# Merged plan of a two-layer diffusion block: the scheduler prices DVE beside GpSimd, and its priorities change

## The chip, the cores and the metric

The kernel runs on one core of a Trainium2 chip. The metric is the device time of one execution in microseconds (us). Engines are named as in the profile: PE is TensorE's matmul, PEld its weight load, DVE is VectorE, ACT is ScalarE, POOL is GpSimd, and SP issues most transfers.

## The reference, cut to what matters

Layer 0 is windowed attention and an MLP, layer 1 a Griffin recurrence and an MLP, over 1024 latent tokens and 256 context tokens of width 1024. The change lies in layer 0's MLP and, above all, in layer 1's recurrent mixer:

```python
def rglru_coeffs(u, w_a, b_a, w_i, b_i, lam):          # five blocks of 256 channels
    r = sigmoid(einsum('btnk,nkj->btnj', ub, w_a) + b_a)
    i = sigmoid(einsum('btnk,nkj->btnj', ub, w_i) + b_i)
    log_a = -LRU_C * softplus(-lam) * r
    return exp(log_a), sqrt(-expm1(2 * log_a)) * (i * u)

def rglru_mixer(h_x, h_c, w_in, conv_w, conv_b, w_a, ..., w_out):
    w_gate, w_rec = w_in[:, :D_RNN], w_in[:, D_RNN:]      # D_RNN = 1280
    u_x = centred_dwconv(h_x @ w_rec, conv_w, conv_b)     # four taps
    u_c = centred_dwconv(h_c @ w_rec, conv_w, conv_b)
    for d in range(2):                                    # two directions
        a_c, bx_c = rglru_coeffs(u_c, ...)
        _, hc_last = linear_scan(a_c, bx_c, 0, rev)       # h = a * h + bx
        a_x, bx_x = rglru_coeffs(u_x, ...)
        ys_x, _ = linear_scan(a_x, bx_x, hc_last, rev)
    return (gelu(h_x @ w_gate) * (ys_x[0] + ys_x[1])) @ w_out
```

Around each mixer and MLP stand RMS norms and adaLN shift, scale and gate.

## The kernel before

Each float32 product is made of three matmuls (lines 249 to 251) of operands split into a high part, which is a rounding copy, and a low part, which is a subtraction. So PE reads nothing that ACT, DVE or POOL has not split first.

No order is written by hand. A `Plan` collects operations with `add`: the engines that may run one, its cost on each, a priority key (lower goes first), what it depends on, and the buffer slots that it takes and frees. `any` adds one that two or three engines may run. `order` walks the list with a clock for each engine: of the operations that can start, it takes the one that starts first, keys deciding among those that start within `eps` of it; a second choice of engine must not end more than `alt` later than the first would; a change of ACT's function table adds `tab` to the key. `cal` scales the costs, and `bus` spaces transfers. `emit` then writes the instructions out in that order, and each engine's instructions run on the chip in the order written, held only by semaphores. An operation of `when` is a pseudo transfer: it moves nothing, and frees slots or delays what depends on it.

There are four plans. The third, merged one holds layer 0's MLP (`layer0_mlp`), layer 1's mixer and the start of layer 1's MLP (`middle`). Its keys are `KEYS2`. In this text:

- u step m (0 to 9), `plan_in`: one 128-channel column of `h @ w_rec`. Three products of PE (tile `pf`, reading `h` and `w`), one for the 256 context tokens (group 2) and one for each latent half (groups 0 and 1); a copy to `prec` and `pre`; the convolution on DVE (lines 1883 and 1887), 12 instructions for a step.
- gate step, `plan_in` too: the same with `w_gate`, gelu on ACT (tile `gp`, line 1921), ten for each latent half.
- block n.d (n 0 to 4, direction d 0 or 1), `plan_rec`: 12 products (tile `pg`, 72 matmuls), 12 sigmoids, exponential, tanh and square root on ACT, the splits of `u` (lines 1958 to 1967), squares, products (lines 2047 to 2079) and scans (line 2087) on DVE, some on POOL.
- output, `plan_proj`: ten groups of eight products with `w_out` (tile `py`), each added into `y` by DVE (line 1681). `plan_residual` and `plan_hgen` then make the next MLP's input (lines 1625 to 1655, and 1579 to 1593), whose first products are `plan_cols` of `middle` and `plan_seven`.

Keys of `KEYS2` used below: u step m has `a0 + ap*m`, its second latent half `al` more; gate steps `g0` or `g1` plus `gp*m`; block n.d `c0 + (2n+d)*cp`; the output `w0`; the next MLP `r0`.

Of the kernel before, what the change touches and what calls it, by code (L numbers as in the profile page):

```python
# [12 lines left out]
ALU = mybir.AluOpType  # L13
# [5 lines left out]
D = 1024  # L19
# [23 lines left out]
class Plan:  # L43
# [4 lines left out]
    def __init__(self, slots, keys, start={}):  # L48
        self.keys = keys
        self.start = start  # L50
        self.free = {s: [(0.0, "DMA", q) for q, m in (n if isinstance(n, list) else [(None, n)]) for _ in range(m)]
                     for s, n in slots.items()}
        self.ops = []
        self.got = {}
        self.cal, self.base = keys.get("cal"), 0.0


    def add(self, eng, ns, key, fn, deps=(), take=(), free=(), tab=None):
        many = not isinstance(eng, str)
# [22 lines left out]
    def order(self):  # L82
# [8 lines left out]
        open_ = {e: [] for e in self.LAT}  # L91
        free = self.free
        tab = None
        bus = 0.0
        for i, o in enumerate(ops):
            if not wait[i]:
                for e, ns in o[0]:
# [2 lines left out]
        eps = self.keys["eps"]  # L100
# [13 lines left out]
        while len(at) < len(ops):  # L114
            best = None
            for e, c in open_.items():
                ts = []
                for i in c:
                    t = first(i, e)
                    if t is None:  # L120
                        continue
                    o = ops[i][0]
                    if len(o) > 1 and o[0][0] != e:
                        if t + dict(o)[e] > first(i, o[0][0]) + o[0][1] + slack:
                            continue
                    ts.append((t, i))
                if not ts:
                    continue
                lim = min(ts)[0] + eps.get(e, 0)
                k, t, i = min((ops[i][1] + (pen if ops[i][6] not in (None, tab) else 0), t, i) for t, i in ts if t <= lim)  # L130
                if best is None or t < best[0]:
                    best = t, i, e
            if best is None:
                raise RuntimeError("plan is stuck: " + str([(ops[i][0], ops[i][1], ops[i][4]) for c in open_.values() for i in c]))
            t, i, eng = best
            opts, key, fn, deps, take, fr, tb, _ = ops[i]
            for e, ns in opts:
                open_[e].remove(i)
            self.got[i] = [(s, free[s].pop(0)[2]) for s in take]
            f = t + dict(opts)[eng]  # L140
            if eng == "DMA" and dict(opts)[eng] >= 2000 and self.keys.get("bus"):
                bus = max(t, bus) + self.keys["bus"] * (1 if dict(opts)[eng] > 2300 else 0.5)
                f = max(f, bus + 1500)
            if tb is not None and tb != tab and eng == "ACT":
                tab = tb
                f += 1283
            if eng != "DMA":
                end[eng] = f
            for x in fr:
# [49 lines left out]
class Body:  # L199
    KEYS = {'ctx': 0.706, 'kv': 0.956, 'q': -1.4, 'S': -0.826, 'dS': 0.182, 'v': 0.068, 'e': 0.292, 'n': -0.211, 'tp': 0.197, 'dt': 0.205, 'a': 0.087, 'pv': 0.593, 'o': 0.343, 'w': 0.695, 'dw': 0.162, 'r': 0.664, 'eps': {'ACT': 143.51971938059006, 'Pool': 265}}  # L200
    KEYS0 = {'cr': 32.6, 'x': [2.69, 4.49, -4.04, -3.82, 11.07, 11.46, 13.54, 8.52, 59.28, 46.73], 'a0': 6.01, 'ad': 4.7, 'ac': 7.11, 'cp': [1, 0, 0, 0, 1, 1, 0, 1, 1, 1, 1, 1, 0, 1, 0, 0], 'w': [2.18, 62.63, 75.38], 'wd': [13.74, 0.3, 15.36], 'h': [-24.73, 13.55, 40.24], 'hd': [3.18, 5.2, 4.18], 'tl': 19.32, 'blocks': [[[0, 1, 2, 3, 4, 5], [6, 7], [8, 9]], [[0, 1, 2], [3, 4], [5, 6], [7, 8, 9]], [[8, 9, 0], [1], [2], [3]]], 'cq': [1, 0, 0, 1, 0, 1, 0, 1, 1, 1, 1, 0, 0, 0, 0, 1, 1, 0, 1, 1, 0, 1, 1, 1], 'p': [32.68, -6.89, 47.14, 3.71, 20.15, -8.8, 64.94], 'pd': 7.27, 'p1': 82.17, 'qk': -8.12, 'k': 144.05, 'g': [45.38, 61.79, 109.14], 'gd': [5.61, 8.84, 15.66], 'alt': 1800, 'eps': {'Q': 0, 'PE': 0, 'Pool': 44, 'DVE': 27, 'ACT': 0}}
    KEYS3 = dict(r=3, alt=200, bus=2300, eps=dict(DVE=100))
    KEYS2 = dict(m=(2.3, 0.68, 10.54), p=(7.5, 1.52, 9.72), h=(10.4, 11.24, 37.3), pi=0.66, a0=28.64, ap=9.33, al=-5.36, g0=155.5,
                 g1=151.7, gp=4.73, c0=98.5, cp=2.33, w0=312.9, wp=16.6, r0=389.52, spill=5, tab=122.87, alt=72.5, ba=8, bb=6, bw=9, bg=7,
                 bo=0, hm=1, cal=1, bus=2300, eps=dict(DVE=20, ACT=0, Pool=48))
# [1406 lines left out]
    def plan_residual(self, p, key, t, ys, yop, xs, xop, G, put, norm):  # L1612
# [25 lines left out]
        for n in range(2):  # L1638
            g.append(p.any(PAIR(512), "DVE Pool", key, lambda e, n=n: e.tensor_tensor(
                out=y(n), in0=y(n), in1=G["G"][:, n * 512:(n + 1) * 512], op=ALU.mult), [sq[n], G["op"]]))  # L1640
            o.append(p.add("DVE", 665, key, lambda n=n: nc.vector.scalar_tensor_tensor(  # L1641
                out=x(n), in0=y(n), scalar=z["a"][:, 2:3], in1=x(n), op0=ALU.mult, op1=ALU.add), [r, g[n], xop]))
        z["g"] = g
        if not norm:
            for n in range(2):
# [207 lines left out]
    def plan_in(self, p, E, h, hop, hold):  # L1853
# [5 lines left out]
        for m in range(NR):  # L1859
# [36 lines left out]
                    tap(i, z["c"][:, 0], z["c"][:, 1])  # L1896
            o = u0 = p.add("DVE", 750, key, c0, [es[1]], take=["t"])
            for i in (0, 1, 3):
                o = p.add("DVE", 1200, key, lambda i=i, z=z, tap=tap: tap(i, z["x"], z["u"]), [o], free=[(es[0], 0)] if i == 3 else [])
            c = p.add("DVE", 1950, key, cc, [es[2]])  # L1900

            def store(m=m, z=z):
# [30 lines left out]
    def plan_rec(self, p, E):  # L1933
# [4 lines left out]
        for n in range(NB):  # L1938
# [32 lines left out]
            for kt in range(2):  # L1971
                lu.append(p.add("DMA", 2500, K - 4, load(kt), deps, take=["t"]))
                c = p.add("DVE", 800, K - 4, split_c(kt), [luc], take=["s"])
                a = p.add("DVE", 605, K - 4, split(kt, 0), [lu[kt]], take=["t"])
                b = p.add("DVE", 1140, K - 4, split(kt, 1), [a], take=["t"])
                uop += [c, a, b]
                uhold += [(c, 0), (a, 0), (b, 0)]
            yt, yhold = {}, {}
            for d in range(2):
# [51 lines left out]
                for jt in range(2):  # L2031
                    for c in (1, 0):
# [28 lines left out]
                        st[jt, c] = p.add("DVE", sz * 1.04 + 70, q, f_st, [b, w_], free=[(w_, 0)])  # L2061
# [7 lines left out]
                for jt in range(2):  # L2069
                    for c in (1, 0):  # L2070
# [143 lines left out]
```

## Time and profile before

| | |
|---|---|
| median of three runs | 2858.9 us (2858.09 to 2860.35) |
| profiled execution: own time, span of its instructions | 2859.99 us, 2858.2 us |
| PE busy | 2673.9 us, 94% of the span |
| DVE busy | 2127.6 us, 74% |
| ACT, POOL busy | 1107.5 us (39%), 851.0 us (30%) |
| mean granted PE clock | 0.972 of full speed |

Shares are means over stages of very different kinds; the merged plan's PE work lies from about 670 to 2243 us. 1.8 us of the execution lie outside the span.

### The profile page before, as it was taken

The numbers are of one execution on the slowest core, as the hardware profiler recorded it, in microseconds if no ns is written. First come the engines' busy times: TensorE is split into PE (matmuls) and PEld (weight loads), VectorE is DVE, ScalarE is ACT, GpSimd is POOL, SyncE is SP. The second block draws the span as 40 slices with busy tenths as digits, with TensorE's granted clock in tenths as the row PEclk, the third lists the DMA queues.
The fourth block names the chain that finished last, engine by engine and source line by source line (L and its number), as shares of the span: only waits on it lengthen the run. The fifth ranks groups of instructions, "written<-read, shape, count | busy, mean of one in ns | idle before, by whom it ended". The sixth has DMA issues, their size and how long they took to land. (4 is left out here: it accounts for less than half of the span.)

```text
span 2858.2 us, 35048 instructions
## 1 busy us (share of the span) xinstructions
PE 2673.9 (94%) x12886; PEld 2205.4 (77%) x12886; DVE 2127.6 (74%) x3178; ACT 1107.5 (39%) x2040; POOL 851.0 (30%) x720
## 2 busy tenths in 40 slices
PE   6798999998999999999998999978896999999997
PEld 4677788877788888888887887756675888888886
DVE  8988999996876666765668677799988666655546
ACT  5326777775322223111115245776525212221111
POOL 7643444443311110100116022355435111101113
PEclk9899999999999999999999999988998999999999
DMA  6462321224233334454552223334331323333323
GB/s 233 157 218 83 110 78 45 68 65 163 74 121 105 129 129 159 155 169 140 168 177 81 92 78 98 136 125 155 139 112 63 110 100 111 133 126 110 102 83 125
DMA packets 115332, 345.03 MB, mean 121 GB/s; under 512 B 12836, under 2 KB 15828, under 8 KB 115160
## 3 DMA queue, kind: packets, MB, share of 16 engines
q1 hardware_dynamic: 111704, 330.21, 34.2%
q10 hardware_dynamic: 3456, 12.58, 1.1%
q8 instruction: 101, 1.65, 0.2%
q14 instruction: 71, 0.58, 0.1%
HBM read 254.37 MB, written 88.38 MB: 120 GB/s over the span
## 5 line engine op out<-in xcount | busy, mean ns | idle before, releaser
L251 PE MATMUL pf<-h,w 128*128 128x512 f32 (+1 forms) x1400 | 517.5, 370 | 23.7 <-POOL w L1525 17.4
L250 PE MATMUL pf<-h,w 128*128 128x512 f32 (+1 forms) x1400 | 516.2, 369 | 9.8 <-DVE h L1593 9.5
L249 PE MATMUL pf<-h,w 128*128 128x512 f32 (+1 forms) x1400 | 516.6, 369 | 5.5 <-ACT h L1583 2.8
L1500 DVE TENSOR_TENSOR y<-y,py 128x512 f32<-128x512 f32 x268 | 183.0, 685 | 274.4 <-PE py L251 273.8
L251 PEld LDWEIGHTS pf<-h,w 128*128 128x128 f32 x1400 | 267.8, 191 | 70.5 <-POOL w L1525 20.0
L250 PEld LDWEIGHTS pf<-h,w 128*128 128x128 f32 x1400 | 267.8, 191 | 56.2 <-DVE h L1593 13.0
L249 PEld LDWEIGHTS pf<-h,w 128*128 128x128 f32 x1400 | 268.0, 191 | 50.7 <-ACT w L244 3.3
L244 ACT CAST w<-raw 128x1024 fp32r<-128x1024 f32 x142 | 148.4, 1049 | 325.2 <-PE pf L251 107.5
L249 PE MATMUL py<-hw,hw 128*128 128x512 f32 x592 | 230.4, 389 | 0.0
L251 PE MATMUL py<-hw,hw 128*128 128x512 f32 x592 | 230.3, 389 | 0.0
L250 PE MATMUL py<-hw,hw 128*128 128x512 f32 x592 | 230.3, 389 | 0.0
L244 ACT CAST hw<-raw 128x512 fp32r<-128x512 f32 x113 | 69.2, 621 | 391.3 <-DMA raw<-in_w 154.3
L1473 POOL TENSOR_TENSOR hw<-raw,hw 128x512 fp32r<-128x512 f32 x46 | 65.3, 1422 | 489.3 <-DVE hw L244 337.9
L1003 POOL TENSOR_SCALAR P<-P,sc 128x640 f32<-128x640 f32 (+2 forms) x160 | 118.5, 753 | 179.7 <-DVE sc L1000 92.2
L249 PE MATMUL py<-w,hw 128*128 128x512 f32 x432 | 169.0, 391 | 0.0
L250 PE MATMUL py<-w,hw 128*128 128x512 f32 x432 | 168.6, 390 | 0.0
L251 PE MATMUL py<-w,hw 128*128 128x512 f32 x432 | 168.4, 390 | 0.0
L1092 PE MATMUL py<-w,oT 128*128 128x512 f32 x480 | 147.5, 412 | 2.5 <-DVE w L927 1.8
L986 ACT ACTIVATE P<-S,sc 128x640 f32<-128x640 f32 (+2 forms) x160 | 113.9, 712 | 52.8 <-DVE sc L980 35.5
L1473 DVE TENSOR_TENSOR hw<-raw,hw 128x512 fp32r<-128x512 f32 x156 | 116.5, 769 | 20.1 <-ACT hw L244 18.4
L249 PEld LDWEIGHTS py<-hw,hw 128*128 128x128 f32 x592 | 111.1, 188 | 23.2
L251 PEld LDWEIGHTS py<-hw,hw 128*128 128x128 f32 x592 | 111.1, 188 | 23.1
(297 smaller groups left out, 6412.7 us busy)
## 6 DMA issues: line engine op xcount, KB each, us to landing
raw<-in_w SPq DMA_DIRECT2D x128, 512.0 KB, 3.5
raw<-in_ada_t SPq DMA_DIRECT2D x96, 512.0 KB, 3.8
raw<-hid_d SPq DMA_DIRECT2D x64, 512.0 KB, 4.0
hid_d<-c SPq DMA_DIRECT2D x112, 256.0 KB, 2.3
raw<-in_w_in SPq DMA_DIRECT2D x30, 512.0 KB
x<-x_d SPq DMA_DIRECT2D x26, 512.0 KB, 5.6
x_d<-x SPq DMA_DIRECT2D x24, 512.0 KB, 2.8
q_d<-qd ACTq DMA_DIRECT2D x20, 512.0 KB, 4.3
```

The source lines that it names most:

```text
L244: (e.copy if e is self.nc.scalar else e.tensor_copy)(out=out, in_=x)
L249: mm(o, lhsT=lh, rhs=rh, start=start, stop=False, skip_group_check=on)
L250: mm(o, lhsT=lh, rhs=rl, start=False, stop=False, skip_group_check=on)
L251: mm(o, lhsT=ll, rhs=rh, start=False, stop=stop, skip_group_check=on)
L986: nc.scalar.activation(out=z["P"][j][:, :n], in_=z["S", j][:, 256:256 + n], func=AF.Exp, scale=0.125, bias=negm[:, j:j + 1], accum_out=l[: ...
L1003: nc.gpsimd.tensor_scalar(out=z["P"][j][:, :n], in0=z["P"][j][:, :n], scalar1=z["sc"][3][:, j:j + 1], scalar2=1.0, op0=ALU.mult, op1=ALU.mult)
L1092: nc.tensor.matmul(z["ps", n], lhsT=oT[k // 2][2]["oT"][:, x, k % 2], rhs=Wo[k][:, w, n * 512:(n + 1) * 512], start=m == 0, stop=m == 3 * ...
L1473: e.tensor_tensor(out=z[n][:, 1], in0=z["raw"][:, s], in1=z[n][:, 0].bitcast(F32), op=ALU.subtract)
L1500: nc.vector.tensor_tensor(out=y, in0=y, in1=z["ps"], op=ALU.add)
```

## The change

`order` learns that a DVE operation with two operands in SBUF takes longer while POOL has an operation of that kind: by up to 0.43 of its cost, and 0.3 of the time that POOL still needs. Operations that DVE or POOL may run are marked by themselves, and some DVE ones by `two=True`. Pseudo transfers no longer count on the bus. The price is in force only in the merged plan, where `cal` is set. `KEYS2` gets other numbers.

```diff
-    def add(self, eng, ns, key, fn, deps=(), take=(), free=(), tab=None):
+    def add(self, eng, ns, key, fn, deps=(), take=(), free=(), tab=None, two=False):
...
+        if two or many and "Pool" in eng and "DVE" in eng:
+            self.two.add(len(self.ops))
...
-            f = t + dict(opts)[eng]
-            if eng == "DMA" and dict(opts)[eng] >= 2000 and self.keys.get("bus"):
+            d = dict(opts)[eng]
+            if i in self.two and self.cal:
+                if eng == "Pool":
+                    pool = t + d
+                elif eng == "DVE" and pool > t:
+                    d += min(0.43 * d, 0.3 * (pool - t))
+            f = t + d
+            if eng == "DMA" and key > -1e8 and d >= 2000 and self.keys.get("bus"):
...
-    KEYS2 = dict(m=(2.3, 0.68, 10.54), p=(7.5, 1.52, 9.72), h=(10.4, 11.24, 37.3), pi=0.66, a0=28.64, ap=9.33, al=-5.36, g0=155.5,
-                 g1=151.7, gp=4.73, c0=98.5, cp=2.33, w0=312.9, wp=16.6, r0=389.52, spill=5, tab=122.87, alt=72.5, ba=8, bb=6, bw=9, bg=7,
+    KEYS2 = dict(m=(1.7, 5.11, -1.71), p=(-1.36, -6.72, 11.35), h=(15.55, 3.89, 35.01), pi=0.41, a0=28.64, ap=3.48, al=16.78, g0=158.15, g1=151.09,
+                 gp=1.49, c0=134.15, cp=4.74, w0=285.16, wp=16.6, r0=353.51, spill=5, tab=541.22, alt=150, ba=7, bb=7, bw=8, bg=9, bo=0, hm=1, cal=1,
...
-                o = p.add("DVE", 1200, key, lambda i=i, z=z, tap=tap: tap(i, z["x"], z["u"]), [o], free=[(es[0], 0)] if i == 3 else [])
+                o = p.add("DVE", 1200, key, lambda i=i, z=z, tap=tap: tap(i, z["x"], z["u"]), [o], free=[(es[0], 0)] if i == 3 else [], two=True)
```

`two=True` also stands at the residual's last addition, at the splits of `u`, and at the recurrence's products and scans. No operation is added or removed. The instructions of the merged plan change their order, and 266 of its operations change their engine. The changed file is ten lines longer where the mixer stands, so a line L2005 of before is L2015 now.

What the scheduler made of it shows at three places. First PE, where block 0.0 begins, before: three rows of a context product of u step 3, then the block's first product, and u step 4 behind a third of the block.

```order
L249 MATMUL pf_14415<-h_13813,w_14306 128x256
L250 MATMUL pf_14415<-h_13813,w_14306 128x256
L251 MATMUL pf_14415<-h_13813,w_14306 128x256
L249 MATMUL pg_14458<-uhc_14381,w_13979 128x256
L250 MATMUL pg_14458<-uhc_14381,w_13979 128x256
L251 MATMUL pg_14458<-uhc_14381,w_13979 128x256
```

The same place of PE's order now: the rows ahead are the last product of u step 9 (a latent half, 512 columns).

```order
L259 MATMUL pf_14996<-h_14115,w_14874 128x512
L260 MATMUL pf_14996<-h_14115,w_14874 128x512
L261 MATMUL pf_14996<-h_14115,w_14874 128x512
L259 MATMUL pg_15039<-uhc_14502,w_13975 128x256
L260 MATMUL pg_15039<-uhc_14502,w_13975 128x256
L261 MATMUL pg_15039<-uhc_14502,w_13975 128x256
```

The recurrence's first product moved behind all ten u steps; gate steps, two to three beside each block, stand between the blocks now, and behind block 3.1 groups of output products.

Second DVE, at the scans of block 0.0 (order prints a scan as a SCALAR_TENSOR_TENSOR of line 2087), before: the convolution of u step 8 still follows them.

```order
L2087 SCALAR_TENSOR_TENSOR gi_2312_14450<-ga_2313_14451,grc_2317_14455,gi_2312_14450 128x1024
L2087 SCALAR_TENSOR_TENSOR gi_2315_14453<-ga_2316_14454,grc_2318_14456,gi_2315_14453 128x1024
L1883 TENSOR_SCALAR prec_15069<-prec_15069,small 128x256
L1887 SCALAR_TENSOR_TENSOR prec_15069<-prec_15069,small 128x254
L1887 SCALAR_TENSOR_TENSOR prec_15069<-prec_15069,small 128x255 x2
L1883 TENSOR_SCALAR u_15150<-pre_15066,small 128x1024
```

DVE at the end of the u steps now: the last convolution of all, two low parts of weights, and then the first products of block 0.0.

```order
L1893 TENSOR_SCALAR u_15067<-pre_14930,small 128x1024
L1535 TENSOR_TENSOR w_15117<-raw_15086,w_15117 128x1024
L2065 TENSOR_TENSOR grc_2367_15037<-grc_2367_15037,uc_14461 128x256
L2065 TENSOR_TENSOR gi_2364_15034<-gi_2364_15034,u_14466 128x1024
L2057 TENSOR_TENSOR gw_15179<-gac_15038 128x256
```

All convolutions stand ahead of the recurrence's products and scans on DVE now; of its work only the splits of the first `u` are earlier.

Third PE again, where block 4.0 begins. Before, a gate step's last product of the second latent half precedes it.

```order
L249 MATMUL pf_16981<-h_14149,w_16945 128x512
L250 MATMUL pf_16981<-h_14149,w_16945 128x512
L251 MATMUL pf_16981<-h_14149,w_16945 128x512
L249 MATMUL pg_17036<-uhc_16851,w_16788 128x256
L250 MATMUL pg_17036<-uhc_16851,w_16788 128x256
```

Now output products (`py`, reading `z`) precede it, the first twenty of them.

```order
L259 MATMUL py_17242<-w_17200,z_16897 128x512
L260 MATMUL py_17242<-w_17200,z_16897 128x512
L261 MATMUL py_17242<-w_17200,z_16897 128x512
L259 MATMUL pg_17261<-uhc_17044,w_16978 128x256
L260 MATMUL pg_17261<-uhc_17044,w_16978 128x256
```

Block 4.0 moved behind two and a half of the ten output groups; before, it stood ahead of all.

## Rows read from the trace of the kernel before

**Rows 1.** The page: granted PE clock in 40 slices of 71.5 us, in tenths.
```profile
PEclk9899999999999999999999999988998999999999
```

**Rows 2.** Windows: length; busy us of PE, PEld, DVE, ACT, POOL; clock; DMA share, GB/s.
```profile
660.00:760.00 100.00, 88.13 (x451) 72.97 (x449) 73.11 (x87) 47.95 (x83) 41.91 (x31) 0.97 0.36 134
760.00:1482.00 722.00, 720.21 (x3494) 609.25 (x3493) 485.01 (x699) 142.07 (x223) 82.36 (x67) 1.00 0.42 139
1482.00:1548.00 66.00, 62.02 (x292) 51.59 (x291) 57.63 (x93) 35.09 (x77) 39.36 (x46) 0.97 0.41 158
1548.00:1615.00 67.00, 62.36 (x321) 52.66 (x320) 50.38 (x66) 23.58 (x39) 14.91 (x13) 0.95 0.28 97
1615.00:1764.00 149.00, 138.91 (x681) 117.08 (x680) 116.18 (x113) 60.83 (x85) 42.73 (x17) 0.97 0.25 86
1764.00:1834.00 70.00, 70.00 (x332) 58.80 (x331) 39.68 (x37) 48.78 (x65) 13.29 (x7) 1.00 0.38 125
1834.00:1898.00 64.00, 53.79 (x226) 42.96 (x225) 60.39 (x55) 47.75 (x63) 26.59 (x15) 0.88 0.34 120
1898.00:1983.00 85.00, 66.07 (x257) 52.19 (x257) 81.03 (x69) 58.15 (x77) 47.26 (x21) 0.83 0.45 154
1983.00:2167.00 184.00, 151.85 (x669) 123.73 (x668) 156.72 (x187) 86.78 (x150) 82.90 (x68) 0.92 0.36 127
2167.00:2243.00 76.00, 67.39 (x290) 54.03 (x288) 56.51 (x63) 30.49 (x49) 29.53 (x18) 0.96 0.13 48
```

**Rows 3.** The waits of PE, 1482 to 2243 us: total, times, longest.
```profile
PE pf L251 <- POOL w L1525: 17.4, 6, 4.7
```

**Rows 4.** PE in order of time: start, length (pipelined: read the starts), operation.
```profile
1482.16 0.39 PE L250 MATMUL py<-hw,hw 128*128 128x512 f32 x1
1482.39 0.39 PE L251 MATMUL py<-hw,hw 128*128 128x512 f32 x1
...
1547.32 0.60 PE L1579 MATMUL ph<-ident,y 128*128 128x128 f32 x4
...
1615.26 0.28 PE L249 MATMUL pg<-uhc,w 128*128 128x256 f32 x1
1615.38 0.28 PE L250 MATMUL pg<-uhc,w 128*128 128x256 f32 x1
```

**Rows 5.** DVE's groups, 1482 to 2243 us: count, busy us, mean ns, idle before.
```profile
L1681 DVE TENSOR_TENSOR y<-y,py 128x512 f32<-128x512 f32 x84 | 56.0, 680 | 15.2 <-PE py L251 14.9
L1525 DVE TENSOR_TENSOR w<-raw,w 128x1024 fp32r<-128x1024 f32 x39 | 52.1, 1339 | 14.0 <-ACT w L244 13.8
L2087 DVE TENSOR_TENSOR_SCAN gi<-ga,grc,gi 128x1024 f32<-128x1024 f32 x10 | 30.0, 3020 | 0.0
L1887 DVE SCALAR_TENSOR_TENSOR u<-pre,small,u 128x1023 f32<-128x1023 f32 x20 | 28.0, 1406 | 0.4
L2079 DVE TENSOR_TENSOR gi<-gi,gr 128x1024 f32<-128x1024 f32 x20 | 27.4, 1375 | 2.4 <-ACT gr L2075 2.4
L1887 DVE SCALAR_TENSOR_TENSOR prec<-prec,small 128x255 f32<-128x255 f32 x20 | 11.9, 595 | 0.7
L1883 DVE TENSOR_SCALAR u<-pre,small 128x1024 f32<-128x1024 f32 x10 | 10.1, 1012 | 16.4 <-ACT pre L244 16.4
L1883 DVE TENSOR_SCALAR prec<-prec,small 128x256 f32<-128x256 f32 x10 | 10.0, 999 | 1.6 <-ACT prec L244 1.1
L1887 DVE SCALAR_TENSOR_TENSOR prec<-prec,small 128x254 f32<-128x254 f32 x10 | 7.2, 723 | 0.4
```

**Rows 6.** One meeting of DVE and POOL, in order of time.
```profile
1737.40 2.60 POOL L1525 TENSOR_TENSOR w<-raw,w 128x1024 fp32r<-128x1024 f32 x1 [5.38 <-ACT w L244]
...
1737.70 3.38 DVE L2079 TENSOR_TENSOR gi<-gi,gr 128x1024 f32<-128x1024 f32 x1
...
1741.94 1.19 DVE L2079 TENSOR_TENSOR gi<-gi,gr 128x1024 f32<-128x1024 f32 x1
```

**Rows 7.** POOL's group of low weight parts, 1482 to 2243 us.
```profile
L1525 POOL TENSOR_TENSOR w<-raw,w 128x1024 fp32r<-128x1024 f32 x15 | 53.9, 3596 | 140.0 <-ACT w L244 118.5 <-DVE w L244 11.6 <-issue 9.0
```

More of the change, by code (lines that the diff above doesn't have):

```diff
@@ L55, in __init__ @@
         self.cal, self.base = keys.get("cal"), 0.0
-    def add(self, eng, ns, key, fn, deps=(), take=(), free=(), tab=None):
+        self.two = set()
+    def add(self, eng, ns, key, fn, deps=(), take=(), free=(), tab=None, two=False):
         many = not isinstance(eng, str)
@@ L93, in order @@
         tab = None
-        bus = 0.0
+        bus = pool = 0.0
         for i, o in enumerate(ops):
@@ L202 @@
     KEYS3 = dict(r=3, alt=200, bus=2300, eps=dict(DVE=100))
-    KEYS2 = dict(m=(2.3, 0.68, 10.54), p=(7.5, 1.52, 9.72), h=(10.4, 11.24, 37.3), pi=0.66, a0=28.64, ap=9.33, al=-5.36, g0=155.5,
-                 g1=151.7, gp=4.73, c0=98.5, cp=2.33, w0=312.9, wp=16.6, r0=389.52, spill=5, tab=122.87, alt=72.5, ba=8, bb=6, bw=9, bg=7,
-                 bo=0, hm=1, cal=1, bus=2300, eps=dict(DVE=20, ACT=0, Pool=48))
+    KEYS2 = dict(m=(1.7, 5.11, -1.71), p=(-1.36, -6.72, 11.35), h=(15.55, 3.89, 35.01), pi=0.41, a0=28.64, ap=3.48, al=16.78, g0=158.15, g1=151.09,
+                 gp=1.49, c0=134.15, cp=4.74, w0=285.16, wp=16.6, r0=353.51, spill=5, tab=541.22, alt=150, ba=7, bb=7, bw=8, bg=9, bo=0, hm=1, cal=1,
+                 bus=2300, eps={'DVE': 20, 'ACT': 50, 'Pool': 50})
     def __init__(self, tc, A, out, dbg=None, stop=None):
@@ L1641, in plan_residual @@
             o.append(p.add("DVE", 665, key, lambda n=n: nc.vector.scalar_tensor_tensor(
-                out=x(n), in0=y(n), scalar=z["a"][:, 2:3], in1=x(n), op0=ALU.mult, op1=ALU.add), [r, g[n], xop]))
+                out=x(n), in0=y(n), scalar=z["a"][:, 2:3], in1=x(n), op0=ALU.mult, op1=ALU.add), [r, g[n], xop], two=True))
         z["g"] = g
@@ L1973, in plan_rec @@
                 c = p.add("DVE", 800, K - 4, split_c(kt), [luc], take=["s"])
-                a = p.add("DVE", 605, K - 4, split(kt, 0), [lu[kt]], take=["t"])
-                b = p.add("DVE", 1140, K - 4, split(kt, 1), [a], take=["t"])
+                a = p.add("DVE", 605, K - 4, split(kt, 0), [lu[kt]], take=["t"], two=True)
+                b = p.add("DVE", 1140, K - 4, split(kt, 1), [a], take=["t"], two=True)
                 uop += [c, a, b]
@@ L2060, in plan_rec @@
                         ex[jt, c] = b
-                        st[jt, c] = p.add("DVE", sz * 1.04 + 70, q, f_st, [b, w_], free=[(w_, 0)])
+                        st[jt, c] = p.add("DVE", sz * 1.04 + 70, q, f_st, [b, w_], free=[(w_, 0)], two=True)
                         iu[jt, c] = p.any(PAIR(sz), "Pool DVE", q, f_iu, [sg[jt, 1, D]] if c else [sg[jt, 1, 0], sg[jt, 1, 512]])
@@ L2081, in plan_rec @@
                         x = p.add("ACT", sz * 0.833 + 93, q, f_sqrt, [st[jt, c]] + list(ex.values()), tab="sqrt")
-                        bb[jt, c] = p.add("DVE", sz * 1.04 + 70, q, f_b, [x, iu[jt, c]], free=[] if c else [own["r%d" % jt]])
+                        bb[jt, c] = p.add("DVE", sz * 1.04 + 70, q, f_b, [x, iu[jt, c]], free=[] if c else [own["r%d" % jt]], two=True)
                     def f_scan(lo, hi, c, jt=jt, view=view, sl=sl, d=d, t=t):
@@ L2091, in plan_rec @@
                     q = K + 3.5 + 0.3 * jt
-                    x = p.add("DVE", 600, q, f_scan(0, 256, 1), [bb[jt, 1]])
+                    x = p.add("DVE", 600, q, f_scan(0, 256, 1), [bb[jt, 1]], two=True)
                     if d == 0:
-                        x = p.add("DVE", 2130, q, f_scan(0, D, 0), [x, bb[jt, 0]], free=[own["a%d" % jt]])
+                        x = p.add("DVE", 2130, q, f_scan(0, D, 0), [x, bb[jt, 0]], free=[own["a%d" % jt]], two=True)
                         sc[jt] = [x, x]
                     else:
-                        x = p.add("DVE", 1140, q, f_scan(512, D, 0), [x, bb[jt, 0]])
-                        sc[jt] = [p.add("DVE", 1140, q, f_scan(0, 512, 0), [x], free=[own["a%d" % jt]]), x]
+                        x = p.add("DVE", 1140, q, f_scan(512, D, 0), [x, bb[jt, 0]], two=True)
+                        sc[jt] = [p.add("DVE", 1140, q, f_scan(0, 512, 0), [x], free=[own["a%d" % jt]], two=True), x]
                 p.when([sc[0][0], sc[1][0]], [own["rc0"], own["rc1"], own["ac"]])
```

## The prediction

> **What bounds the kernel now.** I read the granted clock along the span first: it falls below nine tenths near the start, from 1858 to 2001 us and from 2144 to 2215 us [rows 1]. Then the windows, cut where PE begins a stage [rows 2]. The merged plan begins with 12 us of PE idle in 660 to 760 us; from 760 to 1482 us PE idles 1.8 of 722 us. Whatever the change moves there is hidden by full PE, so the stage from 1482 to 2243 us decides: 761 us.
>
> What must PE do in it? A matmul of 512 columns follows the one before after 0.23 us, one of 256 after 0.12 us [rows 4]; over a long run I take 0.2267. Counted in the order of PE: two hundred and forty matmuls end the old MLP (54.4 us); a u step has 48 wide and 24 narrow ones, 13.8 us; so has a block; a gate step has 24 wide, 5.44 us, twenty of them 108.8; eighty output products of six, 108.8. With the transposes (four take between 0.33, their starts' distance, and 0.60 us [rows 4]) and the next MLP's first products it is 623 us. So 138 of 761 us are lost on PE.
>
> DVE is busy for 619 of the 761 us, the sum of its column [rows 2], and unevenly: 40 of 70 us in 1764 to 1834, where PE is full, but 60 of 64, 81 of 85 and 157 of 184 us from 1834 to 2167, where PE loses 10, 19 and 32 us and the clock is 0.83 to 0.92. In these three windows DVE is the bound; ahead of them PE mostly is. In PE's order of before, ten of the twenty gate steps, which load PE and hardly DVE, stand beside blocks 0.1 and 1.0, and ten are left for the seven later ones.
>
> **What the change does to each stretch.** I worked with two sums. PE's is the count of matmuls above. DVE's: I walked its order, before and now, up to the last instruction that the first matmul of the stretch needs, directly or through others, buffers to be freed included, and gave each instruction the mean of its group [rows 5], the smaller groups in the same way. The stretches end where the block named starts; c1 is the first product of the next MLP. In us, PE / DVE:
>
> - to block 0.0: before 118.2 / 126.3, took 133; now 200.8 / 176.4
> - to block 1.0: before 133.2 / 117.1, took 149; now 71.0 / 69.5
> - to block 2.0: before 69.7 / 52.1, took 70; now 54.8 / 47.4
> - to block 3.0: before 45.2 / 65.2, took 64; now 54.7 / 58.2
> - to block 4.0: before 53.4 / 71.5, took 85; now 65.6 / 94.4
> - to c1: before 141.1 / 167.8, took 184; now 112.6 / 128.5
> - to the end of the plan: before 62.0 / 52.5, took 76; now 63.3 / 63.0
>
> What each stretch took is the length of its windows [rows 2]. The first one grows because all u steps stand ahead of block 0.0: six of them, 6 x 13.8 = 82.6 us of PE. On DVE that brings 15 long taps forward (x 1.36 us, the mean of the rows of 128x1023 and its sister of 128x1022), seven context convolutions ((10.0 + 11.9 + 7.2) / 10 = 2.9 us each), six first taps (1.01), nine low parts of weights (1.22), less 7.6 us of small work that moves the other way: 50 us [rows 5].
>
> In all, DVE's sums come to 652.5 us before and 637.4 now (means of single instructions, which overlap a little with the next: 5% above the busy 619, on both sides). The difference is choices of engine: the low parts of 12 u and gate weights go from POOL to DVE, those of ten weights the other way; eight products of `i` with `u` go to POOL, eleven to DVE; all the rest nets to a few us.
>
> **The sum.** First stretch: PE bounds it now, 200.8 us, and I keep the loss of before, 133 - 118.2 = 14.8 us. 215.6. From block 0.0 to c1 the larger of the two sums, stretch by stretch, is 133.2 + 69.7 + 65.2 + 71.5 + 167.8 = 507.4 before, which took 552 us: 1.088 of it. Now it is 71.0 + 54.8 + 58.2 + 94.4 + 128.5 = 406.9, and x 1.088 that is 442.7. End: 63.3 and the loss of before, 76 - 62, makes 77.3. Together 735.6 us against 761: 25.4 us less. The profiled execution took 2859.99 us, so 2834.6; it lies 1.1 us above the median of the three runs, so about 2834 on their scale.
>
> Costed at nothing: the attention stage, which another plan orders; layer 1's MLP behind the plan, with the same order as before; and 660 to 1482 us. There PE's order changes for a few products, one context product now needing 27 us of DVE work where PE has 25; cover gone, it costs 3 us. Pseudo transfers off the bus let four loads of `xn` and the first MLP weights change places on SP; I take 1 us either way for nothing.
>
> **Bounds.** The loss of the first stretch: between nothing and 30 us, what PE had lost by block 1.0 (133 + 149 - 251.4). Six waits of PE for a low part made by POOL cost 17.4 us before [rows 3], because such a part takes POOL 3.6 us [rows 7] against DVE's 1.3; in the u and gate steps 14 were POOL's and seven are now. Half of that wait may go: -9, taken as nothing. The factor 1.088: from 1.04 to 1.15, inside the spread of the single stretches, 0.98 to 1.19 (-20, +25).
>
> DVE against POOL: in the meeting shown, DVE's product of 128x1024 began 0.3 us after POOL's subtraction and ended 1.1 us after it, 3.38 us where a free one takes 1.19 [rows 6]. It did not slow down, it stood still. The new price would give it 0.43 x 1.2 = 0.5 us at most, against 2.2 lost. The Trainium skill ("SBUF — State Buffer", section "SBUF: two separate sides") says the same: the port pair that the two engines share is locked for a whole instruction, and the other one blocks. By that rule the plan is still too hopeful wherever the two meet, and DVE will come later than the plan puts it. My sum doesn't use the planned times: the means of rows 5 hold the meetings of before. POOL's work beside DVE's from block 0.0 to c1, counted alike, is 0.45 of DVE's before and 0.49 now; if the stretching follows, DVE's sum there grows by 2%, +8 us. If the new keys keep half of the meetings apart, the products of 128x1024 show what is to be had: 1.375 us on the mean where the free one takes 1.19 [rows 5, 6], a seventh of their time; I take a tenth of DVE's sum, -40, as the far end.
>
> **The rivals.** (a) *DVE's backlog, slower.* The u steps leave DVE 24 us of idle time ahead of block 0.0 (200.8 - 176.4), where before two blocks filled it; behind it 398 us of DVE work wait (its sums from 0.0 to c1 without the choice of the larger). If DVE can't be kept fed there, because the sigmoids, square roots and table loads of one block hold up the next, the order loses. It decides at 468 us for that stretch (761 - 215.6 - 77.3), so at DVE rows worth 0.85 of the time. Before, this ratio was 473.7 / 552 = 0.858 over the whole stretch, but 356.6 / 403 = 0.885 from block 1.0 on, and 304.5 / 333 = 0.914 from block 2.0 on, where DVE was really the bound. At 0.82 it would be 485 us, 17 more than before: about 2876. Against it: before each block from 0.0 to 3.1 PE has 20 to 50 us more to do than DVE, counted from 1482, where before the lead sank to nothing by block 3.1; it is gone only at 4.0.
>
> (b) *Nothing changes.* DVE's total falls by 15 us only; were DVE as full over the stage as before (652.5 / 761 = 0.857), the stage would take 744, and with the 8 us of more meetings 752: 9 us less; with a bad first stretch none. 2850 to 2858.
>
> (c) *Much faster.* Meetings kept apart and the waits for POOL's low parts gone: 442.7 - 40 - 9 and the rest as above gives 2785.
>
> **How the numbers follow.** Forecast, 60%: 2834, its own range 2815 to 2850. (c) in part or whole, 14%. (a) 17%. (b) 9%. The range for 8 in 10 goes from 2802 to 2864: it cuts the far ends of (a) and (c). A measurement of this kernel tells about 0.2%, 5.7 us, from no change. Faster by more: the forecast, (c) and a little of (b), 75%; within: 9%; slower: 16%.
>
> **What would show it.** Right: PE nearly full from the first `pf` of the u steps to the first `pg`, which starts some 215 us after the old MLP's last chunk begins; then PE and DVE both over 85% busy, with no window like 1898 to 1983; c1 some 658 us after the same point (before 685); fewer waits of PE for low parts of POOL. Wrong: DVE idle over 12% between first `pg` and c1, waiting for ACT; PE waiting at block 4.0, where the lead is gone, for splits or a freed tile; or DVE's means above those of rows 5.

## The result, and the profile after

The changed kernel takes 2838.4 us (median of four runs, 2834.5 to 2842.6), the one before 2859.6 us in the same comparison (2858.1 to 2862.8): ratio 0.9925, 95% interval 0.9907 to 0.9942, 21 us less. The profiled execution took 2837.45 us, its span is 2835.7.

The granted clock along the span, in 40 slices of 70.9 us: among the blocks it falls below nine tenths in two slices (1914 to 2056 us), as before ([rows 1], 1858 to 2001 us); the slice at the end of the plan, 2144 to 2215 us before, no longer does.

```profile
PEclk9899999999999999999999999998899999999999
```

The windows of the changed kernel, cut where the rows of [rows 2] are cut: the old MLP's last chunk, the u steps, then from block 0.0 to 1.0, 2.0, 3.0, 4.0, c1 and the plan's last product.

```profile
1485.40:1546.90 61.50, 60.04 (x285) 49.51 (x283) 55.14 (x79) 33.24 (x76) 36.71 (x43) 1.00 0.40 149
1546.90:1696.00 149.10, 145.02 (x757) 124.67 (x758) 95.36 (x125) 41.16 (x74) 17.90 (x18) 0.98 0.27 96
1696.00:1772.20 76.20, 73.09 (x338) 60.87 (x337) 65.63 (x58) 54.01 (x71) 31.13 (x14) 0.98 0.36 118
1772.20:1827.70 55.50, 55.19 (x265) 46.13 (x263) 41.25 (x36) 46.39 (x62) 22.35 (x10) 1.00 0.40 132
1827.70:1897.00 69.30, 60.61 (x265) 49.07 (x266) 67.49 (x58) 48.66 (x66) 44.60 (x19) 0.93 0.45 149
1897.00:1991.70 94.70, 72.80 (x313) 58.23 (x312) 94.53 (x86) 66.58 (x95) 48.70 (x26) 0.87 0.37 133
1991.70:2138.30 146.60, 120.21 (x538) 98.05 (x536) 118.44 (x142) 70.61 (x120) 65.73 (x48) 0.92 0.34 117
2138.30:2219.00 80.70, 72.09 (x297) 57.29 (x298) 66.39 (x69) 34.97 (x62) 48.28 (x35) 0.91 0.20 71
sum 733.60, PE 659.05 PEld 543.84 DVE 604.23 ACT 395.60 POOL 315.40; mean PE 82.38 PEld 67.98 DVE 75.53 ACT 49.45 POOL 39.42
```

The stage takes 733.6 us, where it took 760 (1482.6 to 2242.8): 26.6 less. Of that 2.8 us are lost ahead of it, where it now begins at 1485.4, and 1.3 in the MLP behind it (2219.0 to the end, 616.7 us, and 615.4 before). From block 0.0 to c1 it is 442.3 us now, 551.9 before; up to block 0.0 210.6 us, 132.7 before. One window is still as full on DVE as 1898 to 1983 us was: from block 3.0 to 4.0 DVE works 94.5 of 94.7 us and PE 72.8.

PE shows the gain in two halves. Counted to the end of PE's work in the plan, the stage takes 736.0 us against 762.7. PE idles 74.5 us of it against 88.6, and the same 3060 matmuls keep it busy for 661.5 us against 674.1, at a mean granted clock of 0.94 against 0.93.

PE's waits from block 0.0 to c1, longest totals (total, times, longest):

```profile
PE py L259 <- DVE y L1691: 11.7, 3, 7.4
PE pg L259 <- DVE y L1691: 10.9, 1, 10.9
PE pg L259 <- ACT grc L2015: 9.8, 2, 7.0
PE py L260 <- DVE w L1535: 6.2, 1, 6.2
PE pg L260 <- DVE uh L1970: 4.3, 2, 3.1
```

The u and gate products (`pf`), which waited 17.4 us for POOL's low parts of weights [rows 3], do so no longer. What PE waits for most now is DVE. The wait of 10.9 us shows how, in order of time, at block 4.1 (the rows between are left out at the dots):

```profile
2021.66 0.39 PE L261 MATMUL py<-w,z 128*128 128x512 f32 x1
2023.18 7.00 POOL L1535 TENSOR_TENSOR w<-raw,w 128x1024 fp32r<-128x1024 f32 x2
2023.69 8.64 DVE L2097 TENSOR_TENSOR_SCAN gi<-ga,grc,gi 128x1024 f32<-128x1024 f32 x2
...
2032.25 1.85 DVE L1691 TENSOR_TENSOR y<-y,py 128x512 f32<-128x512 f32 x3
2032.96 0.58 PE L259 MATMUL pg<-uhc,w 128*128 128x256 f32 x1 [10.91 <-DVE y L1691]
```

PE's last output product is done at 2022; the addition that takes it out of PE's result tile, 0.7 us of work, stands on DVE behind two scans, and these take 4.3 us each beside two low parts of weights on POOL (3.0 us was their mean before [rows 5]). Until the addition is done, block 4.1 cannot begin.

What DVE itself waits for from block 0.0 to c1, before:

```profile
DVE y L1681 <- PE py L251: 14.7, 25, 0.7
DVE u L1883 <- ACT pre L244: 14.3, 2, 7.2
DVE w L1525 <- ACT w L244: 13.8, 4, 4.2
DVE pre L244 <- PE pf L251: 12.3, 2, 8.0
DVE gi L2055 <- ACT gi L2005: 9.9, 5, 2.5
DVE grc L2055 <- ACT grc L2005: 6.7, 3, 4.1
```

The same now:

```profile
DVE gi L2065 <- ACT gi L2015: 16.5, 7, 3.8
DVE grc L2065 <- ACT grc L2015: 14.4, 6, 3.9
DVE y L1691 <- PE py L261: 6.0, 11, 1.0
DVE w L1535 <- ACT w L254: 3.1, 3, 1.6
```

The two kinds of waits of the u steps (`pre`, `u`: 26.6 us) are gone, since no u step stands between the blocks. Those for weights and outputs fall from 28.5 to 9.1 us; those for sigmoids (`gi`, `grc`) rise from 16.6 to 30.9. DVE idles 551.9 - 453.8 = 98.1 us there before and 442.3 - 387.3 = 55.0 now. In the stretch ahead, where PE is full, DVE now idles 60 us instead of 25; most of that are ten waits for ACT's copy of a u step's context part:

```profile
DVE prec L1893 <- ACT prec L254: 42.9, 10, 7.7
```

So over the whole stage DVE idles 129.5 us now and 142.5 before.

Three of DVE's groups over the stage, and POOL's low parts, which answer to [rows 5] and [rows 7]:

```profile
L1535 DVE TENSOR_TENSOR w<-raw,w 128x1024 fp32r<-128x1024 f32 x41 | 61.6, 1508 | 5.5 <-ACT w L254 5.3
L2097 DVE TENSOR_TENSOR_SCAN gi<-ga,grc,gi 128x1024 f32<-128x1024 f32 x10 | 37.1, 3731 | 0.0
L2089 DVE TENSOR_TENSOR gi<-gi,gr 128x1024 f32<-128x1024 f32 x20 | 24.2, 1214 | 1.5 <-ACT gr L2085 1.5
```

```profile
L1535 POOL TENSOR_TENSOR w<-raw,w 128x1024 fp32r<-128x1024 f32 x13 | 45.1, 3476 | 62.8 <-ACT w L254 33.4 <-DVE w L254 22.6 <-issue 6.8
```

The product of 128x1024 lost its meetings with POOL (1375 to 1214 ns), the scan got them (3020 to 3731), and the low parts of weights got more of them (1339 to 1508). For each DVE instruction of the stage beside which POOL worked I took its time above the median of those of its form beside which POOL did not. The medians are those of all kernels of this document together, since in the changed kernel no scan of 128x1024 was free of POOL. This gives 130 us in sum before and 130 now (two expectations quote 131 and 133, from an earlier count). The new price did not keep the two engines apart.

### The profile page after: what moved, and what is told of

It reads as the page before. It is cut to its first block, busy times and chain, and to the rows that moved or that the text cites. A ratio compares the mean times of both kernels' runs of the same rounds, so it can differ in the third digit from the quotient of the medians.

```text
span 2835.7 us, 35097 instructions
## 1 busy us (share of the span) xinstructions
PE 2664.5 (94%) x12886; PEld 2200.0 (78%) x12886; DVE 2118.4 (75%) x3147; ACT 1114.7 (39%) x2062; POOL 878.4 (31%) x730
## 5 line engine op out<-in xcount | busy, mean ns | idle before, releaser
L1483 POOL TENSOR_TENSOR hw<-raw,hw 128x512 fp32r<-128x512 f32 x52 | 74.0, 1426 | 507.8 <-DVE hw L254 341.8
L1483 DVE TENSOR_TENSOR hw<-raw,hw 128x512 fp32r<-128x512 f32 x150 | 114.6, 786 | 22.6 <-ACT hw L254 20.8
```

What stands on the lines that cost most here:

```text
L1483: e.tensor_tensor(out=z[n][:, 1], in0=z["raw"][:, s], in1=z[n][:, 0].bitcast(F32), op=ALU.subtract)
```

## The experiments

All are compared with the kernel before on the same chip. The first column of times is what that ratio makes of 2860 us, against before; the others come from the profiled executions, cut at the first product of the stage, of block 0.0 and of c1. The last column is the prediction's rule, the sum of the larger of PE's and DVE's sums x 1.088, for the stretch from 0.0 to c1; these sums are counted from the written order, as in the prediction, and no trace shows them. Single executions of one kernel lie up to 5 us from its median, so a difference of a few us between two profiled executions is a hint and no more.

| kernel | ratio (95%) | us | to 0.0 | 0.0 to c1 | DVE busy | DVE idle | rule |
|---|---|---|---|---|---|---|---|
| before | 1 | 0 | 132.7 | 551.9 | 453.8 | 98.1 | 552 |
| changed | 0.9925 (0.9907-0.9942) | -21.4 | 210.6 | 442.3 | 387.3 | 55.0 | 442.7 |
| 1 keys only | 0.9949 (0.9936-0.9961) | -14.6 | 213.6 | 451.5 | 387.3 | 64.2 | 452.8 |
| 2 rule only | 0.9987 (0.9979-0.9996) | -3.7 | 131.4 | 556.8 | 452.5 | 104.3 | 543.7 |
| 3 other keys | 0.9979 (0.9969-0.9988) | -6.0 | 130.3 | 540.2 | 437.2 | 103.0 | 527.8 |
| 4 mixer keys | 0.9964 (0.9951-0.9978) | -10.3 | 215.5 | 458.2 | 394.6 | 63.6 | 472.7 |
| 5 u dose | 0.9964 (0.9951-0.9976) | -10.3 | 219.7 | 446.5 | 395.9 | 50.6 | |
| 6 block dose | 1.0002 (0.9993-1.001) | +0.6 | 212.3 | 463.7 | 409.0 | 54.7 | |
| 7 the same, before | 1.0076 (1.0064-1.0089) | +21.7 | 132.1 | 574.3 | 474.8 | 99.5 | |
| 8 full price | 0.9916 (0.9903-0.993) | -24.0 | 215.4 | 438.8 | 379.2 | 59.6 | 426.6 |
| 9 squares twice, DVE | 0.9981 (0.9972-0.999) | -5.4 | 210.4 | 456.4 | 407.5 | 48.9 | |
| 10 squares twice, POOL | 0.9969 (0.9956-0.9981) | -8.9 | 210.3 | 456.4 | 403.7 | 52.7 | |
| 11 u first | 0.9988 (0.9979-0.9996) | -3.4 | 215.7 | 465.0 | 398.0 | 67.0 | 476.4 |
| 12 squares on ACT | 0.99 (0.9886-0.9913) | -28.6 | 210.3 | 436.9 | 370.7 | 66.2 | |

**1 and 2: the keys, and the rule, each alone.** Kernel before with the new `KEYS2` line; changed kernel with the old one.

> The kernel before with the new numbers of KEYS2 alone; the scheduler has no price for DVE beside POOL and the pseudo transfers stay on its bus. Theory 1 (the order that the keys give, u steps first and gate steps spread, makes the gain): nearly all of the 21 us, 2836 to 2842. Theory 2 (rule and keys need each other, since the keys were fitted to the rule's clock): the larger of PE's and DVE's sums, stretch by stretch, is 680.2 us here, 695.6 before and 670.9 in the changed kernel, so about three fifths of the gain, 16 us, near 2844. Theory 3 (the price makes the gain): no gain, 2855 to 2862.

> The changed scheduler with the old numbers of KEYS2. Theory 1 (the keys' order makes the gain): within 5 us of before, 2855 to 2862. Theory 2 (both are needed): the sum of the larger is 685.5 us, 10 less than before, near 2849. Theory 3 (the price makes the gain): most of it, 2836 to 2842, with fewer or cheaper meetings of DVE and POOL than before (131 us of DVE time lost to them there, 133 in the changed kernel).

The keys alone give 14.6 of the 21.4 us, the rule alone 3.7. Theory 1 is met for the rule; for the keys it is missed, by 5 us of its range. Theory 2's figure for the keys was met (16 expected), that for the rule missed (10). Theory 3 falls: the keys gain most without the price, and DVE's time lost to meetings is 130 us with it, no less than the 125 without it (keys only).

The rule has two parts, the price and the pseudo transfers off the bus, and no run takes them apart. From kernel 1 to the changed one DVE's busy time from block 0.0 to c1 stays at 387.3 us and its idle time falls by 9.2. Kernel 1 has one wait of that size that the changed kernel has not, for the load of the gate `ge`; so what the rule adds to the keys need not come from the price.

```profile
DVE ge L2123 <- DMA ge<-ge_d: 10.5, 1, 10.5
```

**3 and 4: the seven keys that place u steps, gate steps and blocks.** Kernel 3 is the changed kernel with their old values, kernel 4 the one before with their new ones:

```diff
-    ap=9.33, al=-5.36, g0=155.5, g1=151.7, gp=4.73, c0=98.5, cp=2.33
+    ap=3.48, al=16.78, g0=158.15, g1=151.09, gp=1.49, c0=134.15, cp=4.74
```

> The changed kernel with the old values of the seven keys that place u steps, gate steps and blocks (ap, al, g0, g1, gp, c0, cp); the rule and all other new keys stay. Block 0.0 begins between the u steps again, as before. Theory 1 (u steps first and gate steps spread make the gain): the gain goes, 2855 to 2862. Theory 2 (the gain is what the larger of PE's and DVE's sums saves, however the steps lie): the sum is 667.4 us, 3.5 below the changed kernel's, so 2833 to 2838.

> The kernel before with the new values of the same seven keys alone: all u steps stand ahead of block 0.0 and gate steps lie between the blocks, with the old scheduler and the old remaining keys. Theory 1: most of the gain, 2836 to 2843. Theory 2: the sum of the larger is 697.2 us, 1.6 above that of before, so no gain, 2857 to 2863.

Neither theory is met. Taking the seven keys back costs 15 us, where theory 2 had nothing; setting them alone gains 10, where theory 2 had nothing and theory 1 nearly all. The window from block 0.0 to c1 of kernel 3, then of kernel 4:

```profile
1613.70:2153.90 540.20, 476.31 (x2146) 391.02 (x2144) 437.21 (x430) 303.16 (x439) 198.53 (x116) 0.93 0.34 118
```

```profile
1699.60:2157.80 458.20, 387.79 (x1726) 317.55 (x1724) 394.62 (x404) 294.24 (x426) 184.31 (x114) 0.91 0.37 127
```

In kernel 3 DVE has 16.6 us less to do there than before, yet idles 103 us; its wait for the u steps' `pre` alone is 28.3 us, in 4 times:

```profile
DVE u L1891 <- ACT pre L252: 28.3, 4, 8.3
```

In kernel 4 it idles 63.6 us. POOL's busy time in the whole stage is 268 us there against 297, and DVE's time lost to meetings 115 us against 130: my sums, which gave every instruction the mean of before, saw DVE 9 us longer where it was 12 shorter (608 us busy in the stage against 620). So the rule missed kernel 4 because the means don't stay, and kernel 3, as far as these waits show, because of idle time that goes with the order.

**5 to 7: DVE work added, nothing else moved.**

```diff
                 z["u"] = pool.tile([P, D], F32, tag="y", name=self.name("u"))
-                conv0(z["x"], z["u"])
+                for _ in range(4):
+                    conv0(z["x"], z["u"])
```

```diff
-                        nc.vector.tensor_tensor(out=uh[kt, 1], in0=u[kt], in1=uh[kt, 0].bitcast(F32), op=ALU.subtract)
+                        for _ in range(3):
+                            nc.vector.tensor_tensor(out=uh[kt, 1], in0=u[kt], in1=uh[kt, 0].bitcast(F32), op=ALU.subtract)
```

> The changed kernel with the first tap of each latent convolution done four times instead of once (the same values again): thirty more DVE instructions of 0.81 us, 24.3 us of DVE, all ahead of block 0.0; the order of everything else stays. Theory 1 (PE bounds the first stretch, DVE has 200.8 - 176.4 = 24.4 us to spare there): 0 to 8 us more than the changed kernel, 2838 to 2846, and block 0.0 still begins 210 to 218 us after the old MLP's last chunk. Rival (DVE bounds it too, or the backlog that it leaves counts behind block 0.0): 18 to 26 us more, 2856 to 2864.

> The changed kernel with the low part of u, at the start of each block pair, made three times instead of once: twenty more DVE instructions of 1.22 us, 24.4 us, of which 4.9 lie ahead of block 0.0 and 19.5 from there to block 4.0. Theory 1 (the larger of PE's and DVE's sums, stretch by stretch): 4.9 us each to blocks 3.0 and 4.0, 3.4 of the 4.9 to block 1.0, none to 2.0, x 1.088: 14 us more, about 2853. Rival A (DVE is the bound of the whole stretch, whatever the part): 19.5 / 0.90 = 22 us more, about 2860. Rival B (chains through ACT and PE bound it and DVE's fullness is chance): under 8 us more, below 2847.

> The same dose in the kernel before. Theory 1: PE's sum is larger up to block 2.0 and hides it there (16 and 18 us to spare); 4.9 us each to blocks 3.0 and 4.0, x 1.088: 11 us more than before, about 2870. Rival A: 19.5 / 0.86 = 23 us more, about 2882. Rival B: under 6 us, below 2866.

Among the u steps 24.3 us cost 11, and neither theory is met: block 0.0 begins 9.1 us later, counted from the stage's start, and of the added DVE time 8.6 us show behind block 0.0 (395.9 against 387.3), since the last convolutions are not needed for it and slip. PE now waits there for low parts of weights that DVE makes, which it did not in the changed kernel:

```profile
PE pf L261 <- DVE w L1535: 6.1, 6, 1.9
```

So the room there is neither free nor nothing. Among the blocks the dose costs 22 us on either kernel, rival A's figure; theory 1's (14 and 11) and rival B's are missed. In the kernel before, block 1.0 begins 8.3 us later, where PE's sum was 16 us the larger and should have hidden it. Only 2.8 us of that are a wait for the low parts themselves; PE idles 4.9 us more in this stretch and is busy 3.6 us longer, at a clock of 0.95 instead of 0.97. Over the whole stretch from block 0.0 to c1 PE's waits for just these low parts are, before and with the dose:

```profile
PE pg L250 <- DVE uh L1960: 3.7, 3, 1.8
```

```profile
PE pg L250 <- DVE uh L1961: 16.2, 5, 5.4
```

**8: the whole of POOL's remaining time as price.**

```diff
-                    d += min(0.43 * d, 0.3 * (pool - t))
+                    d += pool - t
```

> The changed kernel, but the scheduler charges a DVE operation that begins while POOL has one the whole time that POOL still needs, as the trace shows it, not 0.3 of it. The keys stay as they are. Operations move from DVE to POOL: DVE's sum in the merged plan falls by 50 us, POOL's rises by 51. Theory 1 (the larger of the sums): 656.1 us against 670.9, x 1.088: 16 us below the changed kernel, about 2822. Rival (each operation more on POOL stops DVE as long as POOL works; DVE's means rise by what its count falls): within 5 us of the changed kernel or up to 10 slower, 2833 to 2848, with more than 133 us of DVE time lost to meetings.

Its interval overlaps that of the changed kernel: no difference shown, as the rival said. DVE has 21 instructions less from block 0.0 to c1 but only 8.1 us less busy time, POOL is busy 346 us of the stage instead of 315, and the meetings cost DVE 141 us instead of 130: without them DVE's work in the stage falls by 20 us, and about half of that comes back as meetings, as the rival said. The 3.5 us that the stretch gains are lost ahead of block 0.0, which begins 4.8 us later.

**9 and 10: the squares twice, on DVE and on POOL.** Once with `nc.vector`, once with `nc.gpsimd` for ENGINE:

```diff
-                                e.tensor_tensor(out=t["w", jt, c], in0=a, in1=a, op=ALU.mult)
+                                for _ in range(2 if e is ENGINE else 1):
+                                    e.tensor_tensor(out=t["w", jt, c], in0=a, in1=a, op=ALU.mult)
```

> The changed kernel; each of the 21 squares of the recurrence that DVE makes (twelve of 128x1024, 1.22 us on the mean, nine of 128x256, 0.9 us) is made twice: 22.7 us more of DVE, all between block 0.0 and c1, and not ahead of a block's first product as the low parts of u were. Theory (from there to c1 the time is DVE's work plus a fixed 55 us of idle, whatever is added): 20 to 25 us more than the changed kernel, 2858 to 2864, DVE's idle there 50 to 60 us. Rival (the low parts of u cost so much because PE waits for them at once): under 10 us more, below 2849.

> The changed kernel; each of the 17 squares that POOL makes (six of 128x1024, 2.23 us, eleven of 128x256, 1.06 us) is made twice: 25 us more of POOL, which is busy 212 of the 442 us from block 0.0 to c1. Theory (POOL's work stops DVE, and DVE is the bound): DVE's busy time there grows by more than half of it, and the time by 12 to 22 us, 2851 to 2861. Rival (POOL has time to spare): under 5 us, below 2844.

On DVE 20.2 us more busy time lengthen the stretch by 14.1 (16 us by the ratio): below the 20 to 25 of the theory, above the rival; 6 us come out of DVE's idle time. So the 22 us for the low parts of `u` were in part due to their place, right ahead of a block's products. On POOL the theory holds, at the lower end of its range (12.5 us by the ratio). The window from block 0.0 to c1, changed kernel, then with POOL's squares twice:

```profile
1696.00:2138.30 442.30, 381.90 (x1714) 312.36 (x1712) 387.34 (x376) 286.23 (x412) 212.50 (x115) 0.93 0.37 128
```

```profile
1696.80:2153.20 456.40, 385.09 (x1714) 314.64 (x1712) 403.74 (x376) 286.87 (x412) 235.32 (x132) 0.92 0.36 124
```

DVE does the same 376 instructions and takes 16.4 us longer for them, because POOL works 22.8 us more; the stretch grows by 14.1 us, as with DVE's own squares. POOL is idle half of the time, and yet more work on it is not free.

**11: u steps first, without the gate steps' keys.** Kernel before with four of the seven keys:

```diff
-    ap=9.33, al=-5.36, c0=98.5, cp=2.33
+    ap=3.48, al=16.78, c0=134.15, cp=4.74
```

> The kernel before with new values of four keys (ap, al, c0, cp): all u steps stand ahead of block 0.0, but the output groups stay behind block 4.0 as before. The larger of the two sums, stretch by stretch, is 700.6 us, 5 more than before. Theory (what the change gains is mostly that DVE idles less behind block 0.0 once the u steps are done, 55 to 64 us in three kernels against 98 to 104 in those where they are mixed with it): DVE idle 55 to 70 us from block 0.0 to c1, 2848 to 2854. Rival (the sums by stretch): 2860 to 2867.

DVE's idle time from block 0.0 to c1 is as the theory had it, 67.0 us, but the gain is 3.4 us (its profiled execution was its slowest, 4 us above the median), short of the theory's 6 and far from the rival's loss. What DVE idles less behind block 0.0, 31 us, it idles more ahead of it: 60.8 us there, against 25.0 before. Against kernel 4, which has the new gate step keys too, 7 us are missing: from block 0.0 to 4.0 it takes 16.9 us less, from 4.0 to c1 23.6 more (190.4 and 166.8). Which work that is, was not shown.

**12: DVE's squares on ACT, in the same places.**

```diff
-                            if e is nc.scalar:
-                                e.activation(out=t["w", jt, c], in_=a, func=AF.Square)
+                            if e is not nc.gpsimd:
+                                nc.scalar.activation(out=t["w", jt, c], in_=a, func=AF.Square)
```

> The changed kernel, all instructions in the same places of the program, but the 21 squares that DVE made are made by ACT: 22.7 us less of DVE and 16 us more of ACT (1.04 us for 128x1024), which is busy 286 of the 442 us. Theory (DVE's work plus a fixed idle): 17 to 25 us below the changed kernel, 2813 to 2821. Rival (ACT's chain of sigmoid, exponential, tanh and square root makes DVE's idle time, and lengthens): within 6 us of the changed kernel, 2832 to 2844.

DVE's busy time falls by 16.6 us, the stretch by 5.4. What was taken from its work comes back as waits for ACT's tanh, which now stands behind the squares (in the changed kernel 1.0 us in all):

```profile
DVE gr L2061 <- ACT gr L2049: 7.7, 6, 1.6
DVE grc L2061 <- ACT grc L2049: 7.3, 5, 2.3
```

The theory of a fixed idle time falls for work that is taken away; the rival's 6 us are missed by one. This is the fastest kernel here by its median, 2831.4 us, about 7 below the changed one, but that it is faster is not shown: the intervals just overlap (0.9886 to 0.9913, 0.9907 to 0.9942), and the two stages, 729.1 and 736.0 us to the end of PE's work, differ by the same 7.

## Why the prediction came out, point by point

- **The stage decides; ahead of it and behind it nothing.** Right to 3 us: 2.8 lost ahead, 1.3 behind.
- **First stretch, 215.6 us bounded by PE.** 210.6; PE is busy 145.0 of 149.1 us among the u steps. The loss was 10 instead of 14.8. DVE's sum is too high there, now (176.4 us, where it was busy for 150.5) and before (126.3, busy 107.7): means of the whole stage hold more meetings than this stretch has, where POOL works 54.6 of 210.6 us. The context convolution, 2.9 us by [rows 5], takes 2.0 in the changed kernel. (The nine low parts of weights were put at 1.22 us, where [rows 5] has 1.34; that is 1 us.) So DVE had 60 us of idle time and not 24; but most of it are waits for each u step's result, and kernel 5 shows that 24 us more of work did not fit in free: block 0.0 came 9.1 us later.
- **Block 0.0 to c1, 442.7 us.** Measured 442.3, and an agreement within 1 us is luck. Four of its five stretches were off, in opposite ways: by the rule and as measured 102.7 and 94.7 us from block 3.0 to 4.0, 59.6 and 55.5 from 1.0 to 2.0, 63.3 and 69.3 from 2.0 to 3.0, and 128.5 x 1.088 = 139.8 and 146.6 from 4.0 to c1. In kernels 2, 3, 4, 8 and 11 the rule missed by +13, +12, -14, +12 and -11 us, and the doses of kernels 6 and 7 cost 21 and 22 us there where it had 14 and 11. The step that doesn't hold is that work of the engine with the smaller sum is hidden in its stretch: DVE works ahead in such a stretch, and what it can't do there is missing later. The dose of kernel 6 lengthened the way from 0.0 to 1.0, 2.0, 3.0 and 4.0 by 4.8, 0, 3.8 and 12.1 us, 20.7 in sum, where 4.9 us of work were added to each, 19.5 in sum: by these numbers what 2.0 hid was paid on the way from 3.0 to 4.0, where DVE was busy for 94.5 of 94.7 us without the dose.
- **What the runs show in its place.** The stretch is DVE's busy time plus an idle time that goes with the order: 98 to 104 us in four kernels in which u steps lie between the blocks, 49 to 67 in ten in which they lie ahead. The change took 66.5 us of DVE's work out of the stretch and 43 us of its idle time, and lengthened the one ahead by 78. Of the mixed order's idle time 26.6 us are DVE's waits for u steps (`pre`, `u`); what makes the rest of the difference was not shown.
- **What the order alone does.** It moves DVE's idle time more than it saves it. Over the whole stage DVE idles 142.5 us before, but 143.5 in kernel 4 and 149.2 in kernel 11, where the u steps lie ahead too: what they save behind block 0.0 they lose ahead of it. They gain because DVE is busy 11 to 12 us less; meetings cost it 115 and 111 us there. In the changed kernel 13.7 of the stage's 26.7 us are less DVE busy time, at meetings as before, and 13.0 less idle time. So the gain takes the keys and the rule together; no part of the change that was run alone gives it.
- **Total of DVE, 652.5 to 637.4 by sums.** In busy time 620 to 606 us to the end of PE's work: 14 less, as said.
- **End, 77.3 us.** 80.7; the next MLP's first product starts 9 us behind the last output product, where it was 27 before, and DVE and POOL are busier there (66.4 and 48.3 us, before 56.5 and 29.5).
- **Meetings, taken as unchanged.** 130 and 130 us in the stage: right. The 8 us put down for more of them did not come, though POOL's work beside DVE's from block 0.0 to c1 rose more than said (in busy times from 0.47 of DVE's to 0.55). That the price would be too hopeful was right too (at most 0.3 of the time that POOL still needs, where kernel 10 shows 0.72), but a higher one gained nothing that could be told from the noise (kernel 8): the far end of -40 us was not to be had this way.
- **Waits for POOL's low parts, -9 taken as nothing.** They went (17.4 us for `pf` before), and PE's waits for DVE's additions (`y`, 22.6 us, before 1.7) stand in their place.
- **Rival (a).** DVE's sums fill 397.9 / 442.3 = 0.90 of the stretch; the ratio stayed above the 0.85 below which the order would lose. The marks set for a right forecast came but for the window named below: block 0.0 begins after 210.6 us, PE and DVE are then busy 0.86 and 0.88 of the time, and c1 comes at 652.9 us (658 said). Marks set for a wrong one came too: DVE idles 12.4%, over half of it (30.9 us) waiting for ACT's sigmoids, PE waits 10.9 us for a freed tile at block 4.1, and some of DVE's means lie above those of [rows 5] (the scan, the low parts of weights), others below. The loss that (a) saw is there in part, smaller than the gain. **(b)** fell: DVE is a little fuller over the stage (0.82 of it, 0.81 before), and beside the 14 us less of work this small difference gives 13 more. **(c)** fell with the meetings.
- **Window like 1898 to 1983 gone.** Wrong: 1897 to 1991.7 us is such a one. The change moved DVE's load, it did not level it.

## What to carry to other kernels

Comparing two engines' sums stretch by stretch came within 1.3 us in two of seven kernels here and missed by 11 to 14 in the others. A stretch that "hides" an engine's work only lends the time: add the late engine's work up over the stretches, and ask for its idle time and for what it waits, over the whole stage and not only where it falls. Where two engines stop each other, work moved from the late one to the other is not off its path; measure with a dose of work that changes nothing else. And a dose that is added and one that is taken away need not cost the same: here the one cost 0.7 to 1.1 us of the stretch for a us of DVE, the other gave back 0.3 (0.4 by the medians), because the next engine stood close behind.

## What the runs showed of the hardware

POOL's work costs DVE much of its own length: in kernel 10, 22.8 us more of it made the same 376 DVE instructions 16.4 us longer, 0.72 of it, with DVE busy 0.88 of the time. The Trainium skill ("SBUF — State Buffer", section "SBUF: two separate sides") gives whole-instruction blocking of the shared port pair, for DVE instructions with two SBUF inputs among others; the run agrees with that, though 0.72 alone would not tell blocking from slowing. DVE's instructions of one tensor are hit too: in that run the rounding copies of 128x256 (line 1976) rose from 1034 to 1355 ns on the mean, with the same eight of them.

The granted clock fell behind a wait of PE and came back. Behind the changed kernel's wait of 6.2 us for a low part (`py`, before block 4.0) it is 0.50, the level of 1.2 GHz, and then 0.99 (windows of 4.1 and 2.5 us):

```profile
1985.10:1989.20 4.10, 4.04 (x10) 3.21 (x11) 4.10 (x4) 0.00 (x0) 3.28 (x2) 0.50 0.00 0
1989.20:1991.70 2.50, 2.50 (x12) 2.08 (x11) 2.50 (x5) 0.00 (x0) 0.00 (x0) 0.99 0.84 318
```

So this wait cost twice: the 6.2 us, and ten matmuls that start 0.43 us apart instead of 0.23, 2 us more.
